# Moving k's normalization to GpSimd, and the recurrence's last passes, in a one-core encoder layer

## The chip, the cores and the metric

The kernel runs on one core of one Trainium2 chip. The core has a matrix engine (PE in the profile), a vector engine (DVE), a scalar engine (ACT), GpSimd (POOL), and SyncE (SP), which here only starts transfers. The metric is the device time of one launch in microseconds (us), the median of three runs. Before the change it is 859.28 us (858.77 to 859.71).

## The reference

One layer of a streaming encoder, for 512 positions of 1024 channels, in float32. What matters here, cut from it:

```python
h = rms_norm(x, norm_mix[l])
proj = jnp.einsum('bsd,dc->bsc', h, w_in[l])
u_pool, u_lru, q, k, v, g_logits = jnp.split(proj, splits, axis=-1)
...
qh = rms_norm(q.reshape(B, S, SB_HEADS, SB_HEAD_DIM), q_norm[l])
kh = rms_norm(k.reshape(B, S, SB_HEADS, SB_HEAD_DIM), k_norm[l])
...
# inside rglru_mixer, r and i being two gates of the convolved input xc
log_a = (-LRU_C * r) * jax.nn.softplus(-lru_lambda)
a = jnp.exp(log_a)
mult = jnp.sqrt(-jnp.expm1(2.0 * log_a))
b = mult * (i * xc)
_, h = lax.associative_scan(combine, (a, b), axis=1)      # h[t] = a[t]*h[t-1] + b[t]
```

Three mixers (pooling, the recurrence above, stick-breaking attention over q, k and v with 8 heads of 128) are projected, gated, summed and projected again, and a gated feed-forward block follows. The normalization of k divides each head's 128 values at each position by their root mean square; `k_norm` is folded into q's factor elsewhere in the kernel.

## The kernel before, in words

Float32 products are made from three passes: each weight block is split into a high part (`whi`, rounded to the matrix engine's float32r by ACT, line 141) and a low part (`wlo`, the difference, by DVE, line 142), and so are the activations. A pair of such blocks of 128 x 1024 numbers is called a piece below, and its number is in the tile's name: `whi32` and `wlo32` are piece 32's parts. There are three buffers each for high and low parts, so the high part of a piece can be written once the matrix engine has done with the piece three before it.

The stretch that the change touches makes v, k and q (in this order, `VKQ`). Each is a product with 2 x 2 blocks done by seven block products instead of eight, in the order 11, 12, S2, S1, S3, S4, 22 (`ORDER`); each of the seven uses two pieces, and each piece feeds 12 matmuls (`tok_product`, line 834). So v takes pieces 24 to 37, k 38 to 51 and q 52 to 65; the gates of the third branch follow with pieces 66 to 79. S4's weights are a sum made on DVE at line 209, S2's a difference made at line 214, and S1's and S3's are made by transfers that add to a buffer (GpSimd's queue, lines 200 and 215).

The block results leave the accumulators by ACT (`snap`, line 857) and DVE (`final`, line 865) into tiles `r`. For k each tile (128 x 1024: two blocks of positions, four heads) is then squared and summed on ACT (line 803, 8 instructions), the sums are scaled on DVE (line 810), GpSimd takes the power -0.5 (line 342), four small DVE instructions refine it (lines 343 to 346), ACT multiplies each head by its factor (line 823, 8 instructions), DVE turns the tile (line 814), and GpSimd's queue stores it (line 790). `post`, `post2` and `turn` do this, as background steps that `tick` hands out between pieces.

The recurrence's channels come in four chunks of 256. Chunks 2 and 3 end while v is being made: `lru_decay` (line 701), `lru_input` (709), `lru_scan` (714), `lru_store` (719). They are background steps too.

The order of each engine's instructions is fixed by the compiler from priorities: a split of weights is emitted ahead of its time (`emit_next`, `tc.high_priority`), and `tc.issue_after(x)` keeps an instruction behind x. `los` lists the low parts in the order in which they are emitted.

Of the kernel before, what the change touches and what calls it, by code (L numbers as in the profile page):

```python
# [64 lines left out]
def layer_kernel(ctx: ExitStack, tc: tile.TileContext, x, xt, vecs, w_in, w_qkv7, w_gate7, w_pool, w_rg, w_ig,  # L65
# [125 lines left out]
    def seven_load(n, nms):  # L191
# [3 lines left out]
        for nm in nms:  # L195
            for i in range(pieces):
                qraw[u, nm, i] = r = b4(list(shape), f"qw{u}{nm}{i}", "w")
                nc.sync.dma_start(r, seven_src(u, nm, i))
                if nm == "21":
                    nc.gpsimd.dma_start(r, seven_src(u, "22", i), accum_op=ALU.add)  # L200

    def add_seven(un, nm, i):
        u, pieces, shape = UNITS[un]
        last = i == pieces - 1

        def make(n):
            if nm == "S4":
                r = qraw[u, "12", i]
                dve.tensor_tensor(r, r, qraw[u, "S2", i], ALU.add)
            src = qraw[u, {"S1": "21", "S3": "11", "S4": "12"}.get(nm, nm), i]  # L210
            parts = split_w(src, [P] + list(shape), n)
            if nm == "11":
                qraw[u, "S2", i] = r = b4(list(shape), f"qs{u}{i}")
                dve.tensor_tensor(r, qraw[u, "21", i], src, ALU.add)
                add = nc.gpsimd.dma_start(src, seven_src(u, "21", i), accum_op=ALU.add)
# [221 lines left out]
    with ExitStack() as first:  # L437
# [263 lines left out]
        def lru_decay(c):  # L701
            e, t = lru[c]["r"], lru[c]["t"]
            dve.scalar_tensor_tensor(t, e, 1.0, t, ALU.add, ALU.mult)
            if c < 2:
                dve.tensor_scalar(t, t, -1.0, 1.0, ALU.mult, ALU.add)
            else:
                act(t, t, AF.Identity, scale=-1.0, bias=1.0)

# [10 lines left out]
        def lru_store(c):  # L719
            y = lru.pop(c)["i"]  # L720
            h, l = b4([2, S], f"yh{c}", "b", F32R), y.bitcast(F32R)
            act(h, y, AF.Copy)
            dve.tensor_tensor(l, y, h.bitcast(F32), ALU.subtract)
            for d, t in zip(yd, (h, l)):
                nc.gpsimd.dma_start(d[c // 2][:, 2 * (c % 2):2 * (c % 2) + 2, :], t)
# [53 lines left out]
        gate1(2)  # L779
        for f, c in ((lru_decay, 2), (lru_decay, 3), (lru_input, 2)):  # L780
            step(of(f, c))
# [11 lines left out]
        def post(t, i, j, r):  # L793
# [13 lines left out]
            if t == 0:  # L807
                turn(t, i, j, r, z)
                return
            dve.tensor_scalar(sums, sums, 1.0 / HD, EPS, ALU.mult, ALU.add)  # L810
            bg.append(lambda: post2(t, i, j, r, z, sums))
# [5 lines left out]
        def post2(t, i, j, r, z, s_):  # L817
            y = cst.tile([P, 2, 4], F32, tag="krs", name=f"krs{i}{j}", bufs=2)
            rsqrt(y, s_, (2, 4), f"q{t}{i}{j}")
            for a in range(2):  # L820
                for n in range(4):
                    v = r[:, a, n * HD:(n + 1) * HD]
                    act(v, v, AF.Copy, scale=y[:, a, n:n + 1])
            turn(t, i, j, r, z)


        def q_scales():
# [4 lines left out]
            nc.gpsimd.tensor_scalar(y[1], y[0], -1.0, None, ALU.mult)  # L832

        def tok_product(t, nm, ps, first):
            bh, bl = BQ[WITH[nm]]
            for i in range(2):
                ah, al = weights("seven", t, nm, i)
                tick()
                for a in range(2):
# [9 lines left out]
        for t in VKQ:  # L849
# [25 lines left out]
            for nm in ORDER:  # L875
# [17 lines left out]
                elif nm == "S4":  # L893
                    final((0, 1), ps["S1"])
                else:
                    final((1, 0), ps["22"])
                if (t, nm) == (VKQ[0], "S3"):
                    def last_scan():
                        for j in range(2):
                            with tc.issue_after(los[j - 5]):  # L900
                                lru_scan(3, j)

                    step(of(lru_input, 3)), step(of(lru_scan, 2)), step(last_scan)
                    step(of(lru_store, 2)), step(of(lru_store, 3))
# [899 lines left out]
```

## Time and profile before

| | us |
|---|---|
| median of three runs | 859.28 (858.77 to 859.71) |
| profiled execution | 858.89 |
| its span | 856.8 |
| PE busy in the span | 850.3 |
| DVE busy | 732.3 |
| ACT busy | 533.3 |
| POOL busy | 88.6 |

The span is what the profiler recorded from the first instruction to the last; the execution's time is 2.1 us longer. Busy times add up an engine's instructions, and matmuls that overlap count once. In rows of the timeline the first number is the start, the second how long the instruction took; "xN" says that N like instructions are merged into the row, and in brackets stands how long the engine had been idle and what ended that.

### The profile page before, as it was taken

Reading aid. Unit: us, or ns where it says so; the run is one execution under the profiler, and the core shown is the slowest. Engines: PE = TensorE matmul, PEld = TensorE weight load, DVE = VectorE, ACT = ScalarE, POOL = GpSimd, SP = SyncE. Lnnn points to the kernel's source line nnn. Section 1 sums busy time; section 2 is a strip of 40 time slices with the busy share of each in tenths; the row PEclk is TensorE's granted clock in tenths of the full one; section 3 lists DMA queues with packets and bytes.
Section 4 is the critical chain, followed back from the end, with each engine's and each line's share of the span. In section 5 each row is a group of like instructions: output and inputs, shape, how many; then the busy total and the mean of one; then the engine's idle time right before and its main releaser. Section 6 shows DMA issues by size and latency. Waiting matters only on the chain.

```text
span 856.8 us, 14307 instructions
## 1 busy us (share of the span) xinstructions
PE 850.3 (99%) x5483; PEld 781.2 (91%) x5483; DVE 732.3 (85%) x937; ACT 533.3 (62%) x863; POOL 88.6 (10%) x128
## 2 busy tenths in 40 slices
PE   9999999999999999999999999999999999999998
PEld 7888888888889988889889988889999999999998
DVE  7899898987897699967997877799988888999974
ACT  6554999658887657556665544455655555755642
POOL 1110002123324102000001100000000000121200
PEclk9999999999999999999999999999999999999999
DMA  9586356798585768846668854364533434797913
GB/s 343 160 286 205 101 167 200 215 316 262 141 257 129 228 170 239 246 116 171 174 204 212 182 197 148 99 164 136 145 99 109 114 101 142 221 238 204 199 32 123
DMA packets 141988, 154.09 MB, mean 180 GB/s; under 512 B 41696, under 2 KB 115424, under 8 KB 141920
## 3 DMA queue, kind: packets, MB, share of 16 engines
q1 hardware_dynamic: 129248, 107.30, 40.6%
q0 software_dynamic: 12528, 45.62, 22.5%
q8 instruction: 43, 0.70, 0.3%
q10 hardware_dynamic: 144, 0.26, 0.1%
q14 instruction: 25, 0.20, 0.1%
HBM read 132.71 MB, written 18.87 MB: 177 GB/s over the span
## 4 chain that ended last, share of the span: by engine, by line
PE 88%; ACT 4%; DVE 4%; issue 3%; POOL 1%; DMA 0%; DVEq 0%; POOLq 0%
PE ps_y L315 11%; PE ps_x L315 8%; PE ps_dy L1723 6%; PE ps_q L844 5%; PE ps_dx L1723 5%; PE ps_br L306 3%; PE ps_br L307 3%; PE ps_br L308 3%; PE ps_bY L1347 3%; PE ps_gy L315 3%; PE ps_gate L736 2%; PE ps_bX L1347 2%; PE ps_gx L315 2%; PE ps_pool L308 2%; PE ps_pool L306 2%
## 5 line engine op out<-in xcount | busy, mean ns | idle before, releaser
L141 ACT ACTIVATE whi<-raw 128x1024 fp32r<-128x1024 f32 x69 | 72.9, 1056 | 75.6 <-PE ps_br L307 18.4
L142 DVE TENSOR_TENSOR wlo<-raw,whi 128x1024 fp32r<-128x1024 f32 x69 | 84.2, 1220 | 22.4 <-ACT whi L141 21.9
L142 DVE TENSOR_TENSOR wlo<-qw,whi 128x1024 fp32r<-128x1024 f32 x48 | 58.3, 1220 | 11.6 <-ACT whi L141 11.2
L141 ACT ACTIVATE whi<-qw 128x1024 fp32r<-128x1024 f32 x48 | 50.4, 1052 | 23.6 <-PE ps_q L844 12.8
L1508 ACT ACTIVATE wh_S<-w_S 128x1024 fp32r<-128x1024 f32 x36 | 38.3, 1063 | 28.7 <-PE ps_y L315 20.0
L1629 POOL DMA_DIRECT2D dw<-in_w_down_dram x20 | 17.0, 855 | 305.3 <-DMA dw<-in_w_down_dram 247.7
L1509 DVE TENSOR_TENSOR wl_S<-w_S,wh_S 128x1024 fp32r<-128x1024 f32 x36 | 43.8, 1220 | 3.3 <-ACT wh_S L1508 3.3
L1508 ACT ACTIVATE wh<-w 128x1024 fp32r<-128x1024 f32 x27 | 28.6, 1061 | 28.0 <-PE ps_x L315 9.4
L1509 DVE TENSOR_TENSOR wl<-w,wh 128x1024 fp32r<-128x1024 f32 x27 | 32.9, 1220 | 8.2 <-ACT wh L1508 8.2
L1508 ACT ACTIVATE whdS<-dw 128x1024 fp32r<-128x1024 f32 x20 | 21.2, 1061 | 20.7 <-PE ps_dy L1723 10.6
L1155 DVE TENSOR_TENSOR_SCAN E<-K,ahead 128x512 f32<-128x512 f32 (+3 forms) x32 | 25.4, 814 | 4.6 <-ACT K L1151 4.6
L1509 DVE TENSOR_TENSOR wldS<-dw,whdS 128x1024 fp32r<-128x1024 f32 x20 | 24.3, 1221 | 5.2 <-ACT whdS L1508 5.2
L306 PE MATMUL ps_lru<-HH,whi 128*128 128x512 f32 x64 | 24.6, 384 | 0.0
L306 PE MATMUL ps_br<-yph,whi 128*128 128x512 f32 x64 | 24.4, 382 | 0.0
L306 PE MATMUL ps_gate<-HH,whi 128*128 128x512 f32 x64 | 24.4, 381 | 0.0
L307 PE MATMUL ps_br<-ypl,whi 128*128 128x512 f32 x64 | 24.3, 380 | 0.0
L306 PE MATMUL ps_pool<-HH,whi 128*128 128x512 f32 x64 | 24.3, 379 | 0.0
L306 PE MATMUL ps_br<-yHH,whi 128*128 128x512 f32 x64 | 24.3, 379 | 0.0
L307 PE MATMUL ps_lru<-HL,whi 128*128 128x512 f32 x64 | 24.3, 379 | 0.0
L308 PE MATMUL ps_lru<-HH,wlo 128*128 128x512 f32 x64 | 24.3, 379 | 0.0
L307 PE MATMUL ps_gate<-HL,whi 128*128 128x512 f32 x64 | 24.3, 379 | 0.0
L308 PE MATMUL ps_gate<-HH,wlo 128*128 128x512 f32 x64 | 24.3, 379 | 0.0
(742 smaller groups left out, 3432.1 us busy)
## 6 DMA issues: line engine op xcount, KB each, us to landing
raw<-in_w_in_dram SPq DMA_DIRECT2D x31, 512.0 KB, 5.1
qw<-in_w_qkv_dram SPq DMA_DIRECT2D x24, 512.0 KB, 7.2
dw<-in_w_down_dram POOLq DMA_DIRECT2D x20, 512.0 KB, 7.7
w<-in_w_ffn_gate_dram SPq DMA_DIRECT2D x36, 256.0 KB, 3.9
w<-in_w_ffn_up_dram SPq DMA_DIRECT2D x36, 256.0 KB, 4.1
raw<-in_w_branch_dram SPq DMA_DIRECT2D x16, 512.0 KB, 3.8
qw<-in_w_qkv_dram POOLq DMA_DIRECT2D x12, 512.0 KB, 7.6
g<-gd SPq DMA_DIRECT2D x24, 256.0 KB, 4.5
```

Source lines behind the costliest of these rows:

```text
L141: act(hi, raw, AF.Copy)
L142: los.append(dve.tensor_tensor(lo, raw, hi.bitcast(F32), ALU.subtract).ins)
L306: nc.tensor.matmul(ps, lh, rh, start=start, stop=False, skip_group_check=skip)
L307: nc.tensor.matmul(ps, lh, rl, start=False, stop=False, skip_group_check=skip)
L308: nc.tensor.matmul(ps, ll, rh, start=False, stop=stop, skip_group_check=skip)
L315: nc.tensor.matmul(o, a_[a][:, w, k, :], il2(b_[b][:, k, :]), start=first and n == k == 0, stop=last and n == 2 and k == 3, skip_group_che ...
L844: nc.tensor.matmul(ps[:, a, :], b_[:, k, ts_], il(a_[:, kk, :]), start=first and n == k == 0, stop=n == 2 and k == 3, skip_group_check=True)
L1155: dve.tensor_tensor_scan(E[:, c0:c0 + n][:, ::-1], K[:, c0 + 1:c0 + n + 1][:, ::-1], ahead[:, S - n:][:, ::-1], 0.0, ALU.mult, ALU.add)
L1347: nc.tensor.matmul(o, ah[x_][:, w, k, :], il2(b[k][y_]), start=first_ and n == k == 0, stop=n == 2 and k == 3, skip_group_check=True)
L1508: act(h, src, AF.Copy)
L1509: dve.tensor_tensor(l, src, h.bitcast(F32), ALU.subtract)
L1723: nc.tensor.matmul(o, a_[a][:, w, k0 + k, :], il2(b_[b][:, k, :]), start=first and i == k == 0, stop=last and i == 2 and k == nk - 1, skip ...
```

## The change

- Both chunk pairs of the recurrence now do the affine pass `1 - t` on DVE; before, chunks 2 and 3 did it on ACT.
- The rounding of h for chunks 0 and 1 in `lru_store` goes from ACT to DVE.
- `lru_input` and `lru_scan` of chunks 2 and 3 are no longer all background steps: they are placed by name, each behind a low part of v's products 12, S2 and S1.
- S4's sum on DVE is kept behind the low part of the same unit's S2 piece.
- k's scaling of the sums, the four refining instructions and the multiplication go to GpSimd; the multiplication becomes one instruction of 128 x 1024 with the eight factors broadcast, in place of eight on ACT.
- k's turn on DVE is handed out only when four more low parts have been emitted, and behind the last of them.

```diff
+    seven_lo = {}
+
...
             if nm == "S4":
                 r = qraw[u, "12", i]
-                dve.tensor_tensor(r, r, qraw[u, "S2", i], ALU.add)
+                with tc.issue_after(seven_lo[un, "S2", i]):
+                    dve.tensor_tensor(r, r, qraw[u, "S2", i], ALU.add)
...
             parts = split_w(src, [P] + list(shape), n)
+            seven_lo[un, nm, i] = los[-1]
...
             dve.scalar_tensor_tensor(t, e, 1.0, t, ALU.add, ALU.mult)
-            if c < 2:
-                dve.tensor_scalar(t, t, -1.0, 1.0, ALU.mult, ALU.add)
-            else:
-                act(t, t, AF.Identity, scale=-1.0, bias=1.0)
+            dve.tensor_scalar(t, t, -1.0, 1.0, ALU.mult, ALU.add)
...
-            act(h, y, AF.Copy)
+            if c < 2:
+                dve.tensor_copy(h, y)
+            else:
+                act(h, y, AF.Copy)
...
-        for f, c in ((lru_decay, 2), (lru_decay, 3), (lru_input, 2)):
+        for f, c in ((lru_decay, 2), (lru_decay, 3)):
             step(of(f, c))
...
-            dve.tensor_scalar(sums, sums, 1.0 / HD, EPS, ALU.mult, ALU.add)
+            nc.gpsimd.tensor_scalar(sums, sums, 1.0 / HD, EPS, ALU.mult, ALU.add)
             bg.append(lambda: post2(t, i, j, r, z, sums))
...
-            rsqrt(y, s_, (2, 4), f"q{t}{i}{j}")
-            for a in range(2):
-                for n in range(4):
-                    v = r[:, a, n * HD:(n + 1) * HD]
-                    act(v, v, AF.Copy, scale=y[:, a, n:n + 1])
-            turn(t, i, j, r, z)
+            rsqrt(y, s_, (2, 4), f"q{t}{i}{j}", eng=nc.gpsimd)
+            v = r.rearrange("p a (n d) -> p (a n) d", d=HD)
+            nc.gpsimd.tensor_tensor(v, v, y.rearrange("p a n -> p (a n)").unsqueeze(2).to_broadcast([P, 8, HD]),
+                                    ALU.mult)
+
+            def turn_behind():
+                with tc.issue_after(los[-1]):
+                    turn(t, i, j, r, z)
+
+            due.append((len(los) + 4, turn_behind))
...
                 ah, al = weights("seven", t, nm, i)
+                while due and due[0][0] <= len(los):
+                    due.pop(0)[1]()
                 tick()
...
+                if t == VKQ[0]:
+                    for f, after_ in {"11": ((lambda: lru_input(2), ("12", 0)), (lambda: lru_input(3), ("12", 1))),
+                                      "12": ((lambda: lru_scan(2, 0), ("S2", 0)), (lambda: lru_scan(2, 1), ("S2", 1))),
+                                      "S2": ((lambda: lru_scan(3, 0), ("S1", 0)), (lambda: lru_scan(3, 1), ("S1", 1)))
+                                      }.get(nm, ()):
+                        with tc.issue_after(seven_lo[(0, *after_)]):
+                            f()
                 if (t, nm) == (VKQ[0], "S3"):
-                    def last_scan():
-                        for j in range(2):
-                            with tc.issue_after(los[j - 5]):
-                                lru_scan(3, j)
-
-                    step(of(lru_input, 3)), step(of(lru_scan, 2)), step(last_scan)
                     step(of(lru_store, 2)), step(of(lru_store, 3))
```

Lines of the changed kernel stand a few lower than in the kernel before (line 717 becomes 718, 215 becomes 219, 814 becomes 818).

Three places show how the change moves instructions. The first is DVE's queue while v's S1 and S3 weights are split. `li` is h of the recurrence, `ls` its input and `lt` its decay; `wlo30` and `wlo31` belong to S1, `wlo32` and `wlo33` to S3, `wlo34` and `wlo35` to S4. Before:

```order
L142 TENSOR_TENSOR wlo30_1428<-qw2210_1194,whi30_1427 128x1024
L711 SCALAR_TENSOR_TENSOR ls3_1251<-lr3_1082,ls3_1251 128x1024
L717 SCALAR_TENSOR_TENSOR li2_898<-lt2_1118,ls2_1249 128x512
L142 TENSOR_TENSOR wlo31_1445<-qw2211_1197,whi31_1444 128x1024
L712 TENSOR_TENSOR ls3_1251<-ls3_1251,li3_1083 128x1024
L717 SCALAR_TENSOR_TENSOR li2_898<-lt2_1118,ls2_1249 128x512
L142 TENSOR_TENSOR wlo32_1470<-qw2110_1200,whi32_1469 128x1024
L142 TENSOR_TENSOR wlo33_1486<-qw2111_1202,whi33_1485 128x1024
L717 SCALAR_TENSOR_TENSOR li3_1083<-lt3_1224,ls3_1251 128x512
```

The same place in the changed kernel, where `r200` is the first result tile of v:

```order
L142 TENSOR_TENSOR wlo30_1432<-qw2210_1194,whi30_1431 128x1024
L877 TENSOR_TENSOR r200_1389<-r200_1389,ps_q212_1395 128x1024
L142 TENSOR_TENSOR wlo31_1449<-qw2211_1197,whi31_1448 128x1024
L718 SCALAR_TENSOR_TENSOR li2_898<-lt2_1118,ls2_1249 128x512 x2
L718 SCALAR_TENSOR_TENSOR li3_1083<-lt3_1224,ls3_1251 128x512
L142 TENSOR_TENSOR wlo32_1476<-qw2110_1200,whi32_1475 128x1024
L718 SCALAR_TENSOR_TENSOR li3_1083<-lt3_1224,ls3_1251 128x512
L142 TENSOR_TENSOR wlo33_1492<-qw2111_1202,whi33_1491 128x1024
```

Three scans now stand in a row ahead of `wlo32`, where before there was one right ahead of it; the passes of `lru_input` on `ls3` have gone further up, and one scan now stands between `wlo32` and `wlo33`.

The second place is DVE's queue in the middle of q, where k's tiles are turned (`sq...<-r1..`, STREAM_TRANSPOSE) between the splits of S1's second piece (59) and S3's (60, 61). Before:

```order
L142 TENSOR_TENSOR wlo59_2108<-qw0211_1764,whi59_2107 128x1024
L343 TENSOR_TENSOR krs10_2016<-rsqq110_2017 128x8
L344 TENSOR_TENSOR krs10_2016<-krs10_2016,ssq110_2000 128x8
L345 TENSOR_SCALAR krs10_2016<-krs10_2016 128x8
L346 TENSOR_TENSOR krs10_2016<-krs10_2016,rsqq110_2017 128x8
L142 TENSOR_TENSOR wlo60_2130<-qw0110_1802,whi60_2129 128x1024
L142 TENSOR_TENSOR wlo61_2157<-qw0111_1804,whi61_2156 128x1024
L814 STREAM_TRANSPOSE sq110_1999<-r110_1859 128x1024
```

Now:

```order
L142 TENSOR_TENSOR wlo58_2062<-qw0210_1752,whi58_2061 128x1024
L818 STREAM_TRANSPOSE sq101_1918<-r101_1770 128x1024
L877 TENSOR_TENSOR r000_2023<-r000_2023,ps_q012_2025 128x1024
L142 TENSOR_TENSOR wlo59_2080<-qw0211_1755,whi59_2079 128x1024
L818 STREAM_TRANSPOSE sq110_1976<-r110_1852 128x1024
L142 TENSOR_TENSOR wlo60_2102<-qw0110_1793,whi60_2101 128x1024
```

The four small instructions have left DVE's queue, and the turn of k's last tile (`r110`) has gone from behind `wlo61` to right ahead of `wlo60`.

The third is GpSimd's queue for k's second and third tile (`r111`, `r101`). Before:

```order
L215 DMA qw0110_1802<-in_w_qkv7_dram 128x1024
L342 TENSOR_TENSOR rsqq111_1883<-ssq111_1866,mhalf_82 128x8
L215 DMA qw0111_1804<-in_w_qkv7_dram 128x1024
L342 TENSOR_TENSOR rsqq101_1952<-ssq101_1935,mhalf_82 128x8
L790 DMA qd11_87<-sq111_1865 128x2x512
```

Now:

```order
L814 TENSOR_SCALAR ssq111_1859<-ssq111_1859 128x8
L346 TENSOR_TENSOR rsqq111_1876<-ssq111_1859,mhalf_82 128x8
L347 TENSOR_TENSOR krs11_1875<-rsqq111_1876 128x8
L348 TENSOR_TENSOR krs11_1875<-krs11_1875,ssq111_1859 128x8
L349 TENSOR_SCALAR krs11_1875<-krs11_1875 128x8
L350 TENSOR_TENSOR krs11_1875<-krs11_1875,rsqq111_1876 128x8
L825 TENSOR_TENSOR r111_1809<-r111_1809,krs11_1875 128x1024
L219 DMA qw0110_1793<-in_w_qkv7_dram 128x1024
L814 TENSOR_SCALAR ssq101_1919<-ssq101_1919 128x8
L346 TENSOR_TENSOR rsqq101_1936<-ssq101_1919,mhalf_82 128x8
L347 TENSOR_TENSOR krs01_1935<-rsqq101_1936 128x8
```

Each tile now has seven instructions in a row on GpSimd, and the two transfers that add to q's weights (`qw0110`, `qw0111`) have gone behind the first and into the second of these rows.

More of the change, by code (lines that the diff above doesn't have):

```diff
@@ L832, in q_scales @@
             nc.gpsimd.tensor_scalar(y[1], y[0], -1.0, None, ALU.mult)
+        due = []
         def tok_product(t, nm, ps, first):
```

## The prediction

> **What bounds the kernel now.** I read the page's busy times first, then the matrix engine's waits, then its timeline at each wait.
>
> ```profile
> span 856.8 us, 14307 instructions
> PE 850.3 (99%) x5483; PEld 781.2 (91%) x5483; DVE 732.3 (85%) x937; ACT 533.3 (62%) x863; POOL 88.6 (10%) x128
> ...
> PE ps_q L844 <- DVE wlo L142: 1.5, 4, 0.5
> PE ps_q0S L844 <- DVE wlo L142: 0.2, 1, 0.2
> ```
>
> PE is busy 850.3 of 856.8 us, so little can be won at all. Apart from the start, PE's listed waits are five, all in v, k and q, all for a low part from DVE. Where they are (start, length, idle before):
>
> ```profile
> 143.95 0.48 PE L844 MATMUL ps_q<-wlo,HH 128*128 128x512 f32 x1 [0.29 <-DVE wlo L142]
> 147.35 0.48 PE L844 MATMUL ps_q<-wlo,HH 128*128 128x512 f32 x1 [0.55 <-DVE wlo L142]
> 160.93 0.48 PE L844 MATMUL ps_q<-wlo,hT3h 128*128 128x512 f32 x1 [0.36 <-DVE wlo L142]
> 222.98 0.38 PE L844 MATMUL ps_q<-whi,hT2h 128*128 128x512 f32 x1
> 223.66 0.48 PE L844 MATMUL ps_q<-wlo,hT2h 128*128 128x512 f32 x1 [0.29 <-DVE wlo L142]
> 223.97 0.38 PE L844 MATMUL ps_q<-whi,hT2l 128*128 128x512 f32 x1
> 239.74 0.48 PE L844 MATMUL ps_q0S<-wlo,HH 128*128 128x512 f32 x1 [0.22 <-DVE wlo L142]
> ...
> 171.34 20.72 PE ps_q L844 x96
> ```
>
> These are the second matmuls of pieces 26, 27, 32 (in v), 56 and 62 (in q). Unhindered, a matmul follows the last after 20.72/96 = 0.216 us, so a piece of 12 takes 2.59. At piece 56 the steps are 0.68 and 0.31 in place of twice 0.22: 0.55 lost where the row says 0.29, so a wait costs its idle time and 0.26 more. The five cost 1.7 + 5 x 0.26 = 3.0 us, of which q's two are 0.55 + 0.48 = 1.03.
>
> **v: the low part of piece 32.** DVE works without a pause from the first `lt` pass (line 703) to `wlo32`:
>
> ```profile
> 136.99 1.23 DVE L703 SCALAR_TENSOR_TENSOR lt<-lr,lt 128x1024 f32<-128x1024 f32 x1 [2.54 <-ACT ls L698]
> 159.68 2.33 DVE L142 TENSOR_TENSOR wlo<-qw,whi 128x1024 fp32r<-128x1024 f32 x2
> ...
> 110.29 0.69 DVE L705 TENSOR_SCALAR lt<-lt 128x1024 f32<-128x1024 f32 x1
> 122.67 1.22 DVE L711 SCALAR_TENSOR_TENSOR ls<-lr,ls 128x1024 f32<-128x1024 f32 x1
> 123.92 1.23 DVE L712 TENSOR_TENSOR ls<-ls,li 128x1024 f32<-128x1024 f32 x1
> ```
>
> 159.68 - 136.99 = 22.69 us for the 20 instructions that its queue holds there, 1.134 each. An instruction that needs the result right ahead of it starts 1.25 after (122.67 to 123.92), 0.12 later. The changed queue has 23 from the same pass up to `wlo32`: 21 full ones (the three scans in a row, one more than stood there before) and two affine passes. A full one takes 1.22 and steps by 1.134, so an affine pass of 0.69 steps by about 0.61; `lru_input`'s two passes on chunk 2 now follow each other directly, 0.12. That is 21 x 1.134 + 2 x 0.61 + 0.12 = 25.15 us.
>
> The start moves too. It waits for `ls` from ACT, ahead of which stand the two roundings that leave ACT:
>
> ```profile
> 128.83 1.06 ACT L722 ACTIVATE yh<-li 128x1024 fp32r<-128x1024 f32 x1
> 129.79 1.04 ACT L141 ACTIVATE whi<-qw 128x1024 fp32r<-128x1024 f32 x1
> 132.15 1.04 ACT L722 ACTIVATE yh<-li 128x1024 fp32r<-128x1024 f32 x1
> 133.09 1.51 ACT L695 ACTIVATE lr<-lr,cneg 128x512 f32<-128x512 f32 x2
> 135.90 1.06 ACT L698 ACTIVATE ls<-lt 128x1024 f32<-128x1024 f32 x1
> ```
>
> 0.96 + 0.94 = 1.90 us earlier: 135.09. (The two roundings cost DVE about 0.61 each, inside its 2.54 of idle time; without that cover they would delay everything behind by 1.2.) So `wlo32` starts at 135.09 + 25.15 = 160.24, 0.56 later than now, and PE, which resumed at 160.93, resumes at 161.49. What is won on the way is lost here. Piece 26 is cured: its `wlo26` comes after 5 full steps and 2 affine ones, 135.09 + 6.89 = 141.98, done at 143.20, and wanted at 143.95 - 0.45 = 143.50. `wlo27`, three steps and 0.12 on, is done at 146.7, wanted at 146.09, so about 0.6 stays, although S4's sum no longer stands ahead of it (one pass of `lru_input` does). PE then wants `wlo32` at 143.50 + 6 x 2.59 + 0.7 = 159.7 and waits 1.7. **v's term: +0.56**, whatever the waits ahead of piece 32 come to.
>
> **q: ACT's scalings go.** Before piece 56 and piece 62 ACT held up the high parts:
>
> ```profile
> 218.63 1.85 ACT L823 ACTIVATE r<-r,krs 128x128 f32<-128x128 f32 x6
> 220.39 1.00 ACT L857 ACTIVATE r<-ps_q 128x1024 f32<-128x1024 f32 x1
> 221.29 1.05 ACT L141 ACTIVATE whi<-qs 128x1024 fp32r<-128x1024 f32 x1
> 232.88 0.99 ACT L823 ACTIVATE r<-r,krs 128x128 f32<-128x128 f32 x3 [1.99 <-DVE krs L346]
> ...
> 207.34 0.30 ACT L803 ACTIVATE sq<-r 128x128 f32<-128x128 f32 x1
> 207.83 0.19 ACT L803 ACTIVATION_READ_ACCUMULATOR sq<-r 128x1 f32 x1
> ```
>
> Where six scalings took 1.76 us (218.63 to 220.39), three squares now stand, at 0.34 each (two from 207.34 to 208.02): 1.0. So `whi56` and `wlo56` come 0.7 earlier; they were 0.46 late. Ahead of piece 62 the 1.99 us wait for the factors and eight scalings go and eight squares come: about 2 us, against 0.38 late. DVE sheds the 20 small instructions. **q's term: -1.03**, if nothing new holds DVE.
>
> **GpSimd's chain** is what may. k's last turn stands right ahead of `wlo60` on DVE and waits for GpSimd's product on `r110`; every low part waits behind it.
>
> ```profile
> L342 POOL TENSOR_TENSOR rsqq<-ssq,mhalf 128x8 f32<-128x8 f32 x4 | 8.0, 2001 | 10.1 <-DVE ssq L810 10.0
> L200 POOL DMA_DIRECT2D qw<-in_w_qkv_dram x6 | 5.4, 904 | 18.4 <-DMA qw<-in_w_qkv_dram 18.4
> L345 POOL TENSOR_SCALAR qrs<-qrs 128x32 f32<-128x32 f32 x1 | 1.3, 1278 | 0.1
> L832 POOL TENSOR_SCALAR qrs<-qrs 128x32 f32<-128x32 f32 x1 | 0.3, 301 | 0.1
> L344 POOL TENSOR_TENSOR qrs<-qrs,qss 128x32 f32<-128x32 f32 x1 | 0.3, 253 | 0.1
> L984 POOL MEMSET K<- 128x513 f32 x2 | 1.0, 549 | 0.0
> masks.py:199 POOL TENSOR_SCALAR_AFFINE_SELECT idn<-idn 128x128 f32<-128x128 f32 x1 | 0.3, 282 | 0.1
> ...
> L814 DVE STREAM_TRANSPOSE sq<-r 128x1024 f32<-128x1024 f32 x8 | 9.9, 1241 | 0.5 <-ACT r L823 0.5
> qw<-in_w_qkv_dram POOLq DMA_DIRECT2D x12, 512.0 KB, 7.6
> ```
>
> No row shows a 128x1024 product on GpSimd. Below: a memset of 513 columns takes 549 ns, so 1.1 us for 1024. Above: a 128x32 product takes 253 ns; if none of that were fixed, 8.1 us. The nearest in size is the select on 128x128 float32, 282 ns, eight times which is 2.26. I take X = 2.4. The Trainium skill's page "GPSIMD Engine Reference", section 3.1, has 4497 ns for 2048 elements of a two-input add; half, an estimate of 2.25, would make the sum the same.
>
> A tile's rest: the power 2.0, three small products at 0.25, two two-operation scalings (1.28 each at 32 columns by line 345; a quarter of that if it goes by columns; I take 0.4), six gaps of 0.1: 4.15. `r111`'s squares end at 208.02 + 0.56 = 208.6. Three tiles, two additions and a store at 0.9 in between: 208.6 + 3 x 4.15 + 2.7 + 3X = 223.7 + 3X, or 230.9. PE wants `wlo60` two pieces before 62: 239.36 + 0.56 - 0.55 - 5.18 = 234.2; the turn (1.24) and the split (1.22) need 2.4, so the turn must begin by 231.8. That leaves 0.9 us, and X may reach 2.7. The addition to `qw0110` is issued at about 216 and lands 7.6 later; `whi60` wants it near 229, when its buffer comes free: hidden, and beyond that cover it would cost its lateness in full.
>
> **The sum**: +0.56 - 1.03 = -0.47. Against the profiled 858.89 (856.8 and 2.1 around it) this is 858.4; that execution stood 0.4 under the median 859.28, so on the median's scale **858.8 us**.
>
> **Rivals.**
>
> *All five waits go* (-3.0, 856.3). For it: all five waits are for low parts, and the change touches what stood ahead of each. Against it: the count above; the scans still stand ahead of `wlo32`, and DVE gets about 2.4 us more to do. It needs DVE to start 2.2 us earlier than 135.09.
>
> *GpSimd's chain ends too late* (slower). It decides from X = 2.7, and costs three times what X is above that, since three products follow each other before `r110`'s turn. Six two-operation scalings at 1.28 instead of 0.4 add 5.3, less the 0.9 in hand: +4.4, net +3.9, **863.2**. X = 3.9 with short scalings gives 862.4. For it: 1.28 is the only row of this operation; the power's rows already vary (mean 2.0). Against it: 8 columns, not 32; and the select's row puts X under 2.7.
>
> *DVE and GpSimd hold each other up.* For a trace of both at once:
>
> ```profile
> 266.99 5.79 POOL L342 TENSOR_TENSOR qrs<-qss,mhalf 128x32 f32<-128x32 f32 x1
> 268.72 1.23 DVE L209 TENSOR_TENSOR qw<-qw,qs 128x1024 f32<-128x1024 f32 x1
> ```
>
> A two-input DVE sum inside 5.79 us of GpSimd work keeps its 1.23, so an instruction does not hold DVE as long as it lasts; but it reads only 32 columns. If each of the last two products stops DVE for its whole 2.4 while pieces 56 to 60 are split, the 4.8 less the two or so in hand is at most 2.7; I take half, 1.35: net +0.9, 860.2, which is no change by measure. The Trainium skill says this of such pairs ("SBUF — State Buffer", section "Who interferes with whom": the later of a DVE instruction with two SBUF inputs and a GpSimd one that reads SBUF blocks until the other ends). By that rule the sum is this rival's; the row above does not agree for a short read, and no run here shows a long one.
>
> **Chances.** Forecast 0.50 (its own range 857.8 to 860.6); all waits gone 0.12; chain late 0.28; mutual stops 0.10. The measurement tells about 0.2% (1.7 us) from no change: faster 0.12, same 0.60, slower 0.28. The range runs from 857.0, most of the way to all waits gone, to 863.3, past the chain with long scalings; X near its upper end would go beyond it.
>
> **What would show it.** v: PE's second matmul of piece 32 resumes near 161.5, after three scans; 156 or no wait there would refute the count. q: no waits at pieces 56 and 62, `wlo` done 2 us ahead. GpSimd: the 128x1024 product near 2.4, `r110`'s end before 232; a turn on DVE with idle time ended by POOL, ahead of a waiting `wlo60`, means the second rival; two-input DVE instructions well above 1.22 beside a product mean the third.

## The result, and the profile after

The changed kernel takes **862.84 us** (median of six runs, 861.60 to 864.74) beside 859.20 for the kernel before (858.33 to 859.77): a ratio of 1.0044, with an interval from 1.0029 to 1.0058. It is slower by 3.6 us, where 858.8 was forecast.

The page of the changed kernel, and its matrix-engine waits (total, times, longest). The numbers of its lines have moved by 1 to 12: the accumulation of a block product is now line 856, the turn 818, GpSimd's product 825.

```profile
span 860.9 us, 14287 instructions
PE 850.7 (99%) x5483; PEld 780.5 (91%) x5483; DVE 735.2 (85%) x921; ACT 521.2 (61%) x827; POOL 108.4 (13%) x152
...
PE ps_q L856 <- DVE wlo L142: 4.3, 4, 1.9
PE ps_q0S L856 <- DVE wlo L142: 0.5, 1, 0.5
```

PE has as much to do as before; the listed waits for low parts have grown from 1.7 to 4.8 us. The time is in two stretches, which the table by windows shows (PE's busy time is the second number). The kernel before:

```profile
120.00:180.00 60.00, 58.80 (x274) 50.06 (x273) 55.30 (x50) 45.54 (x52) 14.18 (x20) 1.00 0.79 245
180.00:250.00 70.00, 69.49 (x320) 59.95 (x320) 56.76 (x67) 56.97 (x169) 16.67 (x15) 1.00 0.79 232
```

The changed kernel:

```profile
120.00:180.00 60.00, 58.11 (x272) 49.52 (x271) 57.52 (x53) 41.53 (x48) 13.99 (x20) 1.00 0.77 235
180.00:250.00 70.00, 67.03 (x308) 57.33 (x307) 55.95 (x46) 47.92 (x131) 35.43 (x40) 1.00 0.78 228
```

v (the first row) lost 0.7 us of PE, k and q lost 2.5. Where it stands still, from its timeline (with 0.26 to add to each bracket, as in the prediction):

```profile
146.96 0.48 PE L856 MATMUL ps_q<-wlo,HH 128*128 128x512 f32 x1 [0.59 <-DVE wlo L142]
161.65 0.48 PE L856 MATMUL ps_q<-wlo,hT3h 128*128 128x512 f32 x1 [1.30 <-DVE wlo L142]
219.75 0.48 PE L856 MATMUL ps_q<-wlo,HH 128*128 128x512 f32 x1 [0.57 <-DVE wlo L142]
233.52 0.48 PE L856 MATMUL ps_q0S<-wlo,hT1h 128*128 128x512 f32 x1 [0.53 <-DVE wlo L142]
238.23 0.48 PE L856 MATMUL ps_q<-wlo,hT3h 128*128 128x512 f32 x1 [1.85 <-DVE wlo L142]
```

These are pieces 27 and 32 in v, and 54, 59 and 60 in q (219.75 lies in the third of q's pieces). A smaller loss has no bracket: the second matmul of piece 49, at 205.97, comes 0.40 us after the first. Pieces 26, 56 and 62, which waited before, do not wait any more. What stands ahead of the low parts that are late in q, on DVE:

```profile
203.56 1.25 DVE L818 STREAM_TRANSPOSE sq<-r 128x1024 f32<-128x1024 f32 x1 [2.33 <-POOL r L825]
217.06 2.65 DVE L142 TENSOR_TENSOR wlo<-qw,whi 128x1024 fp32r<-128x1024 f32 x1
224.88 1.22 DVE L142 TENSOR_TENSOR wlo<-qs,whi 128x1024 fp32r<-128x1024 f32 x1
226.02 2.92 DVE L212 TENSOR_TENSOR qw<-qw,qs 128x1024 f32<-128x1024 f32 x1
235.82 1.25 DVE L818 STREAM_TRANSPOSE sq<-r 128x1024 f32<-128x1024 f32 x1 [2.36 <-POOL r L825]
236.99 2.32 DVE L142 TENSOR_TENSOR wlo<-qw,whi 128x1024 fp32r<-128x1024 f32 x2
```

Two things: two turns that wait 2.3 us for GpSimd, the first right ahead of `wlo49` and the second right ahead of `wlo60`; and two-input instructions that take 2.65 us (`wlo54`) and 2.92 us in place of 1.22. GpSimd's side of it:

```profile
211.49 0.19 POOL L814 TENSOR_SCALAR ssq<-ssq 128x8 f32<-128x8 f32 x1 [5.58 <-ACT sq L807]
213.51 1.28 POOL L347 TENSOR_TENSOR krs<-rsqq 128x8 f32<-128x8 f32 x1
214.87 1.20 POOL L348 TENSOR_TENSOR krs<-krs,ssq 128x8 f32<-128x8 f32 x1
216.16 0.20 POOL L349 TENSOR_SCALAR krs<-krs 128x8 f32<-128x8 f32 x1
216.72 1.90 POOL L825 TENSOR_TENSOR r<-r,krs 128x1024 f32<-128x1024 f32 x1
225.10 2.76 POOL L825 TENSOR_TENSOR r<-r,krs 128x1024 f32<-128x1024 f32 x1
233.89 1.90 POOL L825 TENSOR_TENSOR r<-r,krs 128x1024 f32<-128x1024 f32 x1
```

The long DVE instructions overlap a product: the split at 217.06 ends 1.09 us after the product that ran from 216.72 to 218.62, as if it had begun only then. The other way round, an instruction on 128x8 takes 0.20 us alone and 1.28 and 1.20 us in the two rows where it meets a two-input DVE instruction (1.22 us), and the product of 2.76 began at 225.10, within the split that ran from 224.88 to 226.10. So each holds the other up for the rest of an instruction. The Trainium skill ("SBUF — State Buffer", section "Who interferes with whom") has a DVE instruction with two SBUF inputs and a GpSimd instruction that reads SBUF exclude each other. These rows agree; the long power of the prediction's third rival, beside which a DVE sum kept its 1.23, had misled me.

### The profile page after: what moved, and what is told of

The parts are those of the page before. It is cut to its first block, busy times and chain, and to the rows that moved or that the text cites. A ratio compares the mean times of both kernels' runs of the same rounds, so it can differ in the third digit from the quotient of the medians.

```text
span 860.9 us, 14287 instructions
## 1 busy us (share of the span) xinstructions
PE 850.7 (99%) x5483; PEld 780.5 (91%) x5483; DVE 735.2 (85%) x921; ACT 521.2 (61%) x827; POOL 108.4 (13%) x152
## 4 chain that ended last, share of the span: by engine, by line
PE 80%; issue 7%; DVE 6%; ACT 4%; DMA 2%; POOL 1%; SPq 0%; DVEq 0%; ACTq 0%; POOLq 0%
PE ps_y L319 11%; PE ps_x L319 8%; PE ps_dy L1736 6%; PE ps_q L856 5%; PE ps_dx L1736 5%; PE ps_br L311 3%; PE ps_br L312 3%; PE ps_br L310 3%; PE ps_bY L1360 2%; PE ps_gy L319 2%; DVE wlo L142 2%; PE ps_bX L1360 2%; PE ps_gate L740 2%; PE ps_gx L319 2%; PE ps_lru L310 1%
## 5 line engine op out<-in xcount | busy, mean ns | idle before, releaser
L1522 DVE TENSOR_TENSOR wldS<-dw,whdS 128x1024 fp32r<-128x1024 f32 x20 | 24.3, 1221 | 5.2 <-ACT whdS L1521 5.2
L311 PE MATMUL ps_br<-yHL,whi 128*128 128x512 f32 x64 | 24.4, 381 | 0.2 <-DMA yHL<-ydl 0.2
L311 PE MATMUL ps_br<-ypl,whi 128*128 128x512 f32 x64 | 24.3, 380 | 0.0
L310 PE MATMUL ps_pool<-HH,whi 128*128 128x512 f32 x64 | 24.3, 379 | 0.0
L310 PE MATMUL ps_br<-yHH,whi 128*128 128x512 f32 x64 | 24.3, 379 | 0.0
L311 PE MATMUL ps_lru<-HL,whi 128*128 128x512 f32 x64 | 24.3, 379 | 0.0
L312 PE MATMUL ps_lru<-HH,wlo 128*128 128x512 f32 x64 | 24.3, 379 | 0.0
L311 PE MATMUL ps_gate<-HL,whi 128*128 128x512 f32 x64 | 24.3, 379 | 0.0
```

What stands on the lines that cost most here:

```text
L310: nc.tensor.matmul(ps, lh, rh, start=start, stop=False, skip_group_check=skip)
L311: nc.tensor.matmul(ps, lh, rl, start=False, stop=False, skip_group_check=skip)
L312: nc.tensor.matmul(ps, ll, rh, start=False, stop=stop, skip_group_check=skip)
L1522: dve.tensor_tensor(l, src, h.bitcast(F32), ALU.subtract)
```

## The experiments

All times below are medians; each kernel stood beside runs of the kernel before on the same chip, and the ratios and intervals are against those. The edits are to the changed kernel unless said otherwise. The expectations were written before each run and count one piece too far in two places: what they call the wait at piece 55 is at piece 54, and the one at piece 64 is at piece 65.

**1. GpSimd's part alone.** The recurrence's part is undone, the rest stays:

```diff
-            dve.tensor_scalar(t, t, -1.0, 1.0, ALU.mult, ALU.add)
+            if c < 2:
+                dve.tensor_scalar(t, t, -1.0, 1.0, ALU.mult, ALU.add)
+            else:
+                act(t, t, AF.Identity, scale=-1.0, bias=1.0)
...
-        for f, c in ((lru_decay, 2), (lru_decay, 3)):
+        for f, c in ((lru_decay, 2), (lru_decay, 3), (lru_input, 2)):
...
```

> The change without its recurrence part (affine passes and roundings back on ACT, lru_input and lru_scan as background steps again); k's normalization on GpSimd, the later turn and the place of S4's sum stay. Theory G (GpSimd's chain for k's tiles, lengthened by its conflicts with DVE, holds the turns on DVE and costs about 3.0 us in k and q; the recurrence part costs 0.6 in v): 859.2 + 3.0 = 862.2, with the turn ahead of wlo60 still waiting for GpSimd's product and wlo32 done near 160.9 as before the change. Rival R (the recurrence part and its knock-on make most of the loss): within 0.8 of before, 859 to 860.

Measured: 862.25, ratio 1.0036 [1.0024, 1.0048]. PE's waits in q are those of the changed kernel to 0.01 us (54, 59 and 60), those in v are those of before. So nearly the whole loss is GpSimd's part (with S4's sum placed as in the change).

**2. The recurrence's part alone,** with the S4 sums behind the S2 low parts, and k normalized as before:

```diff
-            nc.gpsimd.tensor_scalar(sums, sums, 1.0 / HD, EPS, ALU.mult, ALU.add)
+            dve.tensor_scalar(sums, sums, 1.0 / HD, EPS, ALU.mult, ALU.add)
...
-            rsqrt(y, s_, (2, 4), f"q{t}{i}{j}", eng=nc.gpsimd)
...
+            rsqrt(y, s_, (2, 4), f"q{t}{i}{j}")
+            for a in range(2):
+                for n in range(4):
+                    v = r[:, a, n * HD:(n + 1) * HD]
+                    act(v, v, AF.Copy, scale=y[:, a, n:n + 1])
+            turn(t, i, j, r, z)
```

> The change without its GpSimd part: k's sums, refinement and scaling where they were (DVE and ACT), the turn not put off; the recurrence part and the place of S4's sum stay. Theory G: v loses 0.6 as in the change (PE resumes at piece 32 near 161.5), q's waits stay about as before the change, so 859.2 + 0.6 = 859.8, between 859.2 and 860.5. Rival R: 862 or more.

Measured: 863.87, ratio 1.0050 [1.0038, 1.0063]. The expectation fell: this is no better than the whole change. From its PE and ACT timelines:

```profile
226.58 0.79 PE L848 MATMUL ps_q<-whi,hT2h 128*128 128x512 f32 x1 [3.52 <-ACT r L861]
227.59 0.63 PE L848 MATMUL ps_q<-whi,hT2l 128*128 128x512 f32 x1
...
218.65 1.86 ACT L827 ACTIVATE r<-r,krs 128x128 f32<-128x128 f32 x6 [2.27 <-DVE krs L350]
221.37 1.84 ACT L827 ACTIVATE r<-r,krs 128x128 f32<-128x128 f32 x6
224.06 1.26 ACT L827 ACTIVATE r<-r,krs 128x128 f32<-128x128 f32 x4
225.53 1.00 ACT L861 ACTIVATE r<-ps_q 128x1024 f32<-128x1024 f32 x1
```

ACT's copy out of the accumulator, for which PE waits, stands behind 16 scalings; before it stood behind six, at 220.39. PE stood 3.5 us and then ran its matmuls at half the pace for a while. What moved the copy is the next experiment's question.

**3. The same without the S4 place:**

```diff
-                with tc.issue_after(seven_lo[un, "S2", i]):
-                    dve.tensor_tensor(r, r, qraw[u, "S2", i], ALU.add)
+                dve.tensor_tensor(r, r, qraw[u, "S2", i], ALU.add)
```

> The kernel of e2_recurrence_only with one thing less: the S4 sums stand where the kernel before has them, not behind the S2 low parts. In e2 TensorE waited 3.5 us in q for ScalarE's copy r<-ps_q, which stood behind ten more scalings than before, and its matmuls then took 0.63 instead of 0.38 us for 2.7 us. Theory: it is the S4 place that put that copy behind the scalings; with it undone the copy stands behind six scalings again, q's two waits are as before, and only the recurrence's price is left: three waits of together 2.55 us at pieces 27, 30 and 32 against 2.07 before, 0.5 us: 860.1 (859.6 to 860.6) beside a kernel before of 859.6. Rival: the recurrence itself moves ScalarE's order in q; then the wait of 3.5 us stays and the time is 863.9 as in e2.

Measured: 859.05, ratio 1.0005 [0.9996, 1.0014]. The copy stands behind six scalings again and the long wait is gone: shown, it was the S4 place, through the compiler's order of ACT. The recurrence's part by itself makes no difference that can be told. The time lies 0.55 below the range I gave, mostly because the kernel before also took 0.4 less beside it (859.21 where I had 859.6). v's three waits are 0.70, 0.49 and 1.24 us, 2.4 against 2.0 before, so the price that I put at 0.5 is 0.4, less than the interval can show.

**4. The turns later:** every turn put off by seven low parts instead of four.

```diff
-            due.append((len(los) + 4, turn_behind))
+            due.append((len(los) + 7, turn_behind))
```

> The change with k's turn put off by seven low parts instead of four; nothing else. Theory G: the turns find GpSimd's product done, the waits of 2.3 us on DVE ended by POOL go, and with them PE's waits at pieces 49 and 60 (0.3 + 2.1) and the late start of the second tile; what conflicts of DVE and GpSimd cost by themselves (PE's waits of 0.8 at pieces 55 and 59) may stay: 859.0 to 860.6. If the conflicts alone make the loss and not the turns' waits, it stays within 1 us of the change, 862 to 863.

Measured: 860.25, ratio 1.0008 [1.0000, 1.0017], as expected. No turn waits for GpSimd any more, and the waits at 49, 59 and 60 are gone. One is left in q, at piece 54, and grew to 1.2 us. On DVE, at the first tile's product and ahead of piece 54, and GpSimd's product there:

```profile
201.72 2.93 DVE L142 TENSOR_TENSOR wlo<-qw,whi 128x1024 fp32r<-128x1024 f32 x1 [0.45 <-ACT whi L141]
...
216.36 4.58 DVE L142 TENSOR_TENSOR wlo<-qw,whi 128x1024 fp32r<-128x1024 f32 x2
...
216.80 1.92 POOL L825 TENSOR_TENSOR r<-r,krs 128x1024 f32<-128x1024 f32 x1
```

Two splits that take 2.32 us elsewhere take 4.58 beside that product. So putting the turns off wins back some 3 us. The waits at 49 and 60, 2.4 us by PE's steps, stood right behind turns that waited; the 0.8 at 59 stood behind the sum of 2.92 us, which meets no product here; the wait at 54 grew by 0.4. What is left is 0.5 more in v, and in q 1.2 for the 1.0 that the change cured; that 1.2 is what reaches PE of the hold-up of DVE by the product.

**5. GpSimd's part alone with the turns at seven** (the kernel of experiment 1 with the edit of 4):

> The kernel of e1_no_recurrence (GpSimd's part alone, the recurrence as before) with the turns at 7 instead of 4. Theory: e1's loss is the turns' waits for GpSimd plus the low part beside a product; at 7 only the latter is left, as in e3 (1.2 us at piece 55), and the three waits in v are those of before (2.0): 3.2 us of waits against 3.0 to 3.3 before: 859.4 (858.8 to 860.2), no difference. Rival: GpSimd's part costs more than its waits: 860.5 or above.

Measured: 859.46, ratio 1.0002 [0.9993, 1.0011], as expected. GpSimd's part is neither a gain nor a loss once its turns come late enough.

**6. Only the first tile's turn later.** Which made the last product late: the first turn, which held DVE, or the length of GpSimd's own work?

```diff
-            due.append((len(los) + 4, turn_behind))
+            due.append((len(los) + (7 if (t, i, j) == (1, 0, 0) else 4), turn_behind))
```

> The changed kernel with one number changed for one tile: only the first tile's turn (of k's r100) is put off by 7 low parts, the other three by 4 as in the change. In the changed kernel this turn held VectorE 2.33 us for GpSimd's first product; the sums of the second tile came to GpSimd at 211.49 and the last product ended at 235.79, 4 us later than the turn behind it could bear. In e3, with all turns at 7, the sums came at 210.20 and the last product still ended at 235.57. Theory: the lateness is mostly GpSimd's own length (four tiles in 24 to 25 us against the 20.8 that the prediction's own rows give with a product of 1.90), not the first turn; so the last product still ends at 235 or later, the wait at piece 60 stays above 1.2 us, and only the waits at 49 (0.28) and part of that at 60 go: 862.0 (861.3 to 862.8). Rival: the first turn starts it all; then the chain moves forward by about 2 us, the waits at 59 and 60 fall below 0.5 us, and the time is 860.3 (859.8 to 860.9).

Measured: 863.36, ratio 1.0048 [1.0034, 1.0061]. From its GpSimd and DVE timelines:

```profile
210.21 0.20 POOL L814 TENSOR_SCALAR ssq<-ssq 128x8 f32<-128x8 f32 x1 [6.64 <-ACT sq L807]
234.04 1.90 POOL L825 TENSOR_TENSOR r<-r,krs 128x1024 f32<-128x1024 f32 x1
...
229.57 1.25 DVE L818 STREAM_TRANSPOSE sq<-r 128x1024 f32<-128x1024 f32 x1 [1.79 <-POOL r L825]
235.97 1.25 DVE L818 STREAM_TRANSPOSE sq<-r 128x1024 f32<-128x1024 f32 x1 [2.92 <-POOL r L825]
```

The sums come 1.28 us sooner and the last product ends at 235.94, no sooner than 235.79. The rival (the first turn starts it all) is out as it was forecast. But the edit moved one thing more: the store of the first tile, put off with its turn, now stands ahead of the second tile's product, and GpSimd does nothing else from 215.65 to 216.79. That costs 1.1 us, and the small instructions 0.3 more (13.9 us for the 18 of the last three tiles, 13.6 in the changed kernel). The time is above what I expected, because the waits moved instead of going: by PE's steps 1.2 us at piece 54, 0.3 at 59 and 2.7 at 60, 4.2 in all where the changed kernel has 4.0. The profiled execution, at 865.52 the longest of the five, also lost clock behind the last of them (below); the median one did not.

**7. The refinement on DVE, the product on GpSimd:**

```diff
-            nc.gpsimd.tensor_scalar(sums, sums, 1.0 / HD, EPS, ALU.mult, ALU.add)
+            dve.tensor_scalar(sums, sums, 1.0 / HD, EPS, ALU.mult, ALU.add)
...
-            rsqrt(y, s_, (2, 4), f"q{t}{i}{j}", eng=nc.gpsimd)
+            rsqrt(y, s_, (2, 4), f"q{t}{i}{j}")
```

> The change with the scaling of the sums and the four refining instructions back on DVE; GpSimd keeps the power and the 128x1024 product, turns at four as in the change. Theory G with short instructions to blame (they take 1.2 to 1.5 us instead of 0.2 beside two-input DVE work): GpSimd's chain for a tile falls from about 5.2 to 2.5 us, r110 is done some 6 us earlier, the turns wait no more: 859.0 to 860.6. If the product alone is to blame, the turns still wait and it stays near 862.

Measured: 866.14, ratio 1.0073 [1.0061, 1.0086]. The expectation fell. From DVE's timeline:

```profile
216.54 0.17 DVE L347 TENSOR_TENSOR krs<-rsqq 128x8 f32<-128x8 f32 x1 [1.57 <-POOL rsqq L346]
219.34 0.15 DVE L350 TENSOR_TENSOR krs<-krs,rsqq 128x8 f32<-128x8 f32 x1
219.81 1.76 DVE L349 TENSOR_SCALAR krs<-krs 128x8 f32<-128x8 f32 x1
222.84 1.98 DVE L142 TENSOR_TENSOR wlo<-qw,whi 128x1024 fp32r<-128x1024 f32 x1
```

The short instructions are shorter here, but they stand in DVE's queue among the splits: the first waits 1.57 us for GpSimd's power, the fourth of the same tile comes 2.8 us behind it, after an addition and a split, and one of them, beside a product, takes 1.76. GpSimd's chain did get as short as I said:

```profile
227.61 2.81 POOL L825 TENSOR_TENSOR r<-r,krs 128x1024 f32<-128x1024 f32 x1 [0.89 <-DVE krs L350]
```

This is `r110`'s product, and it ends at 230.4, 5.4 us earlier than in the changed kernel; only the first turn still waits (1.79 us). So the small instructions on GpSimd do make the chain late. But PE now loses 1.5, 2.8, 1.0 and 0.5 us at pieces 54, 55, 57 and 59. What I left out, as I read these rows, is that a round trip between two queues costs the place in each.

**8. The product in pieces, with one tensor input** (the edit of 4, and eight instructions on 128x128 with one number per partition):

```diff
-            nc.gpsimd.tensor_tensor(v, v, y.rearrange("p a n -> p (a n)").unsqueeze(2).to_broadcast([P, 8, HD]),
-                                    ALU.mult)
+            for n in range(8):
+                nc.gpsimd.tensor_scalar(v[:, n, :], v[:, n, :], y[:, n // 4, n % 4:n % 4 + 1], None, ALU.mult)
```

> The kernel of e3_turn_at_7 with GpSimd's product of two tensors (1.90 us) replaced by eight products of 128x128 with one number per partition, as one-tensor instructions. In e3 VectorE's pair of low parts at 216.36 took 4.58 instead of 2.36 us while a product ran. Theory: any GpSimd instruction of this size keeps VectorE's two-input instructions waiting while it runs: the pair still takes 3.4 us or more and the time is that of e3, 860.3 (859.8 to 861.5). Rival: it is the two inputs on GpSimd's side that exclude; then the pair takes 2.4 us, the wait at piece 55 goes and the time is 859.1 (858.7 to 859.6).

Measured: 869.12, ratio 1.0128 [1.0109, 1.0147]; neither forecast holds: the pair at piece 54 takes 1.29 and 1.22 us and its wait is gone, as the rival had it, but PE stops for 4.6 us at piece 60. GpSimd's eight, early and late:

```profile
201.67 8.80 POOL L826 TENSOR_SCALAR r<-r,krs 128x128 f32<-128x128 f32 x8
232.55 4.67 POOL L826 TENSOR_SCALAR r<-r,krs 128x128 f32<-128x128 f32 x8
```

With DVE idle (5.15 us ahead of its turn at 237.25) they take 4.67 us, 0.58 each, and up to 8.80 beside a busy DVE, against 1.90 for the one product. DVE's splits take 1.3 us at most, so here such a short instruction holds them up by 0.1 us at most. So it is not the two inputs on GpSimd's side that exclude: with one it waits too, and there are eight starts at which it can. The chain gets longer by that, and the turn ahead of `wlo60` waits the 5.15 us.

**9. The recurrence taken apart.** With the turns at seven (the kernel of 4), v's waits are the greater part of what is left. Each was a pass of 1.14 us too many ahead of a low part (three scans ahead of `wlo32`), so no more than two are left ahead of any:

```diff
-                with tc.issue_after(seven_lo[un, "S2", i]):
+                with tc.issue_after(seven_lo[(un, "S2", i) if un else (0, *(("S2", 1), ("S3", 0))[i])]):
...
+                    for f, c, nx in {"11": ((lru_input, 2, "12"),), "12": ((lru_input, 3, "S2"),),
+                                     "S1": ((lru_scan, 2, "S3"),), "S3": ((lru_scan, 3, "S4"),)}.get(nm, ()):
+                        for j in range(2):
+                            with tc.issue_after(seven_lo[0, nx, j]):
+                                f(c, j)
```

(`lru_input(c, j)` now makes one of its two passes.)

> The kernel of e3_turn_at_7 with the recurrence's late work taken apart: the two passes of each input and the scans one at a time behind ever later low parts (S2, S3, S4 instead of two together behind 12 and three together behind S1), the two S4 sums of v behind the second S2 and the first S3 low part. Theory: TensorE's waits at pieces 27, 30 and 32 (0.82, 0.17 and 1.56 us in e3) are VectorE passes of 1.14 us each that stand ahead of a low part; with at most two ahead of each they go, and the one wait left in v, k and q is that at piece 55 (1.2): 860.25 - 2.55 = 857.7 (857.3 to 858.6). Rival: VectorE is full there, and the waits only move to the later pieces: 859.5 to 860.5.

Measured: **857.31**, ratio 0.9974 [0.9965, 0.9983]: faster than both kernels. By windows:

```profile
120.00:180.00 60.00, 60.00 (x284) 51.92 (x283) 58.27 (x54) 42.41 (x50) 14.90 (x20) 1.00 0.82 248
180.00:250.00 70.00, 69.09 (x328) 60.39 (x327) 60.59 (x49) 51.11 (x147) 38.64 (x42) 1.00 0.79 231
```

PE does not stand still in v at all, though DVE does more there than before (58.27 us of 60).

**10. The same spreading without GpSimd's part** (the kernel of experiment 3, taken apart in the same way):

> The kernel of e5_recurrence_without_S4_place (the recurrence's part alone, no GpSimd part) with v's passes, scans and S4 sums taken apart as in e6. Theory: the gain of e6 over the kernel before is this spreading; the three waits in v (0.70, 0.49 and 1.24 us in e5) go, q's two (0.55 and 0.47) stay: 859.05 - 2.43 = 856.6 (856.1 to 857.4), no slower than e6 with GpSimd's part. Rival: the spreading pays only beside GpSimd's part; then 858.5 or above.

Measured: 857.70, ratio 0.9983 [0.9975, 0.9992]. Faster than before as well, by 1.7 us instead of the 2.6 expected: v's waits are all gone, but that at piece 56 has grown from 0.55 to 1.0 us. Its interval overlaps that of experiment 9, so whether GpSimd's part adds anything there stays open; the spreading is what pays.

**11 and 12. The wait at piece 54.** The kernel of 9 with all turns put off by 11, and with only the first one:

```diff
-            due.append((len(los) + 7, turn_behind))
+            due.append((len(los) + 11, turn_behind))
```

```diff
-            due.append((len(los) + 7, turn_behind))
+            due.append((len(los) + (11 if (t, i, j) == (1, 0, 0) else 7), turn_behind))
```

> As e6_turn_at_7_spread, with the turns put off by 11 low parts instead of 7. In e3 the first tile's turn (1.14 us) stands among the nine VectorE instructions without a gap before the low part of piece 55, which comes 1.2 us late; at 11 it stands behind it. Theory: the wait at 55 goes as well: 1.1 us less than e6, 856.6 (856.2 to 857.4), with no wait in v, k and q above 0.3 us. Rival: GpSimd's product and VectorE's low part exclude each other whatever is ahead, and the wait stays or comes back one piece later: as e6.

> As e6_turn_at_7_spread, with only the first tile's turn put off by 11 low parts and the others by 7. In e7, where all were put off by 11, the wait at piece 55 went, but GpSimd's queue then held a weight load behind the stores of the late turns (VectorE idle 2.97 us before qs at 242.99) and TensorE waited 0.8 us at piece 64 and 1.8 us for ScalarE's gx at 255.0. Theory: with the other turns where e6 has them this load is in time, and only the wait of 1.2 us at piece 55 goes: 857.31 - 1.17 = 856.1 (855.7 to 857.0). Rival: the wait at 55 is the exclusion of low part and product itself and comes back a piece later: as e6, 857.3.

Measured: 858.93, ratio 0.9993 [0.9984, 1.0002], and 858.80, ratio 0.9988 [0.9979, 0.9998]. In both the wait at piece 54 is gone, and in both PE waits elsewhere instead. With all turns at 11, from the DVE timeline and the waits:

```profile
242.99 1.23 DVE L218 TENSOR_TENSOR qs<-qw,qw 128x1024 f32<-128x1024 f32 x1 [2.97 <-DMA qw<-in_w_gate_dram]
...
PE ps_gy L319 <- ACT gx L949: 1.6, 1, 1.6
```

With only the first one at 11, DVE:

```profile
230.40 3.45 DVE L142 TENSOR_TENSOR wlo<-qw,whi 128x1024 fp32r<-128x1024 f32 x2
244.43 1.23 DVE L218 TENSOR_TENSOR qs<-qw,qw 128x1024 f32<-128x1024 f32 x1 [3.79 <-DMA qw<-in_w_gate_dram]
```

In the first PE waits at piece 65 (0.8) and in the next stage. In the second q reaches the last product sooner, and now that one holds up the splits of pieces 60 and 61 (3.45 for 2.32); the product before it holds up a sum ahead of piece 59. The two cost PE 0.6 and 0.8 us. And DVE idles 3.79 us for a load of weights that stands between stores in GpSimd's queue (issued at 233.15, awaited until 244.43), which makes piece 65 late by 1.1. So the second's rival held in that the hold-up comes back, though later and at a higher price than it said (858.80 for 857.3): while DVE has no slack, a product that holds it for 2 us is paid somewhere.

## Why the prediction was wrong

**The step that failed** is "GpSimd's chain": `r110`'s product was to end at 230.9, 0.9 us ahead of need. It ended at 235.79, and its turn waited 2.36 us. The difference of 4.9 has two parts.

The start: I let the chain begin with `r111`'s squares, moved by v's term alone, to 208.6; the sums came at 211.49. The first tile, whose turn I counted as free, is what is missing. In the changed kernel DVE waits 2.33 us for its product at 203.56, and what follows on DVE (the addition into `r111`, so the squares) is late by that; in experiments 4 and 6 that turn is out of the way, yet the sums still come at 210.20 and 210.21, behind a split that the same product stretches to 2.93 (the first row of experiment 4). So of the 2.9 us the turn's place makes 1.3; the other 1.6 stay with the turn out of the way, because the first product then holds up a split instead.

The length: from the sums of `r111` to the end of `r110`'s product 24.3 us, where I had 22.3. The product was not the fault, though it was the term I bounded at length: 1.90, 2.76 and 1.90, a mean of 2.19 where I had taken 2.4 and where the rival was to decide from 2.7. The other six instructions of a tile were: 4.74, 4.13 and 4.72 us without gaps, where I had 3.55. Alone they take 2.7 (1.67 for the power, five at 0.20); eight of the 18 took longer. The row of 1.28 us that I read as the possible price of a two-operation scaling was such a meeting (it ran from 273.52, a split on DVE from 273.50), and so is not the operation's price. The same instruction in the changed kernel:

```profile
278.60 0.22 POOL L349 TENSOR_SCALAR qrs<-qrs 128x32 f32<-128x32 f32 x1
```

**The sum had no term for DVE beside a product.** I left that hold-up to the third rival, at 0.10. It is the 0.82 and 0.79 us of new waits at pieces 54 and 59, behind the instructions of 2.65 and 2.92 us.

**v's term** was right: +0.56 forecast. `wlo32` began at 160.40 where 160.24 was said, behind the 23 instructions that I counted, and let PE go on at 161.65 where 161.49 was said; against 160.93 before, less 0.12 by which this execution started late, that is +0.60. Piece 26 is cured, 27 still waits (0.85 for 0.6). Experiment 9 bears the reading out: with the scans apart the waits go.

**q's term** was right as far as it went: no wait at pieces 56 and 62 in the changed kernel. But the new ones at 49, 54, 59 and 60 come to 0.28 + 0.82 + 0.79 + 2.11 = 4.0 us, by PE's steps. With v's 0.6, less the 1.03 cured, that is 3.6 us, the measured loss.

**The rivals.** The second (the chain ends too late, 863.2) has the sign, the place and nearly the time of what happened, with a chance of 0.28. That its time comes so near is luck, and so is it that the range, drawn up to it, holds 862.84: its 5.3 us were six dear scalings, which there were not. Its cause is the third's: DVE and GpSimd hold each other up. I gave the two separate prices, when the one is how the other comes about. The "two or so in hand" that the third rival counted against the hold-up of DVE were not there at piece 54: DVE had seven instructions in a row ahead of its split in experiment 4, with no gap between them, so of a hold-up of 2.3 us 1.2 reached PE.

## What to carry to other kernels

Before work goes to GpSimd, look at what DVE does in the same microseconds: beside two-input work on DVE, each instruction can be lengthened by the rest of the other's, so price a chain of short GpSimd instructions at a DVE instruction for every start that may meet one, and a long one at its full length in DVE's queue. An instruction that waits for another engine is worth putting off until that engine is surely done, since everything behind it in its queue waits too, but not past what the next stage needs from the same queue. Where an in-order engine is nearly full, spread its side work one at a time between the instructions that the bound engine waits for: that gained here what neither half of the change did.

## What I had not expected of the hardware

A stop of PE can cost more than its length. By windows of 4 us the granted clock (the third number from the end) after the stop of 2.42 us in the profiled execution of experiment 6:

```profile
234.00:238.00 4.00, 1.96 (x10) 1.37 (x8) 2.03 (x2) 3.52 (x13) 3.96 (x4) 1.00 0.55 207
238.00:242.00 4.00, 3.62 (x10) 2.96 (x11) 3.72 (x4) 0.00 (x0) 1.12 (x2) 0.65 0.98 174
242.00:246.00 4.00, 4.00 (x19) 3.40 (x18) 1.90 (x2) 1.73 (x2) 0.00 (x0) 0.93 1.02 393
```

The clock lost is 4 x 0.35 + 4 x 0.07 = 1.7 us, which is half the clock for 3.4 us. Around stops of 2.42, 2.55 and 3.52 us (experiments 6, 7 and 2) matmuls followed each other in 0.43 us instead of 0.22 for some 3 us, which cost about 1.6 us each time, and around one of 4.63 us (experiment 8) for 6 us. Around the 1.85 us of the changed kernel the clock stayed at 1.00 in the profiled execution. The Trainium skill ("TensorE: Matmul & The Clock Gate", section "Why this matters for your kernels") warns of idle gaps above about 3 us; these traces show the drop for shorter ones.

The length of the stop does not decide alone. Half the clock for 3.4 us of 862 makes a mean of 0.998, and each execution has its mean on record. Two of the six executions of the changed kernel show 0.998 (863.93 and 864.74 us; the other four take 861.60 to 863.01), two of six in experiment 1, which has the same stop, two of five in experiment 6 (864.94 and 865.52; the others 862.67 to 863.36), three of five in experiment 7, and all five in experiments 2 and 8 0.998 or less. In experiments 3 to 5 and 9 to 11, whose profiled executions have no stop above 1.63 us, none shows less than 0.999. So with the same kernel the clock falls in one execution and not in the next; where in those executions it fell, and what decides, these runs do not show.
